# MLP products of a two-layer encoder as pairs of 64-row products in the two row halves of TensorE's array

## The chip, the core and the metric

The kernel runs on one core of a Trainium2 chip. The metric is the device time of the whole program in microseconds (us). The core's engines are TensorE (PE in the profile, its weight loads PEld), VectorE (DVE), ScalarE (ACT), GpSimd (POOL) and SyncE (SP, which here only issues transfers); each works through its own list of instructions and waits on semaphores for the others.

## What is computed

A two-layer encoder trunk on one sequence of 512 tokens, model width 1024, MLP width 4096, all in float32. Each layer is a mixer (layer 0: sparse attention beside gated linear attention; layer 1: stick-breaking attention) and then an MLP. The change touches the MLP alone:

```python
def squared_relu_mlp(n, w_up, w_down):
    return jnp.square(jax.nn.relu(n @ w_up)) @ w_down

# in each of the two layers
h = h + mixer(rmsnorm(h, g_mix[layer]), ...)
h = h + squared_relu_mlp(rmsnorm(h, g_ffn[layer]), w_up[layer], w_down[layer])
```

## The kernel before

The activations lie feature-major: a tile is 128 features on the partitions by all 512 tokens, so `h` is eight tiles and the MLP's hidden layer 32. One product on TensorE takes 128 x 128 weights as the operand that stays and a 128 x 512 tile as the operand that streams, and adds into one PSUM bank of 128 x 512 float32. For accuracy every float32 operand x is split into two tiles of the type float32r, hi and lo with hi + lo = x, and a product is made in three passes, hi·hi, hi·lo and lo·hi (`mm3`). ScalarE makes hi by a copy, VectorE makes lo by a subtraction (`split`).

Weights come in blocks of 128 x 1024 (half a megabyte): `plan` lists them in the order in which they are used, SP loads `raw`, ScalarE makes `whi` and VectorE `wlo`, with three buffers of each. `proj_fm` takes one block and makes eight `mm3`, 24 products, into one bank.

`mlp` runs in two halves of the hidden layer. For each of 16 hidden tiles f it calls `proj_fm` on the eight normed tiles of `h`, and the bank goes through ReLU (ScalarE), a square (VectorE) and a split. Then for each of the eight output tiles d it calls `proj_fm` twice on the 16 hidden tiles (48 products in one bank), VectorE multiplies the bank by the norm's factor `r2` and adds it to `h[d]`. In the second half `nxt(d)` follows: the norm's split for layer 1, or the store of the output. That is 2 x (16 x 24 + 8 x 48) = 1536 products in one MLP and 3072 in the two, all of one shape. The factor `r2` comes from `mean_fm`: a sum of squares is gathered tile by tile on POOL (`sum_squares`) and summed over the partitions by two products with a tile of ones, `ones_r`, which stand among the first products of the MLP.

The order of the instructions on each engine isn't that of the code. Each call is recorded by `Program.add`, and `Program.issue` makes a list schedule from the costs in `Program.cost`: of the instructions whose inputs are there, an engine takes the one of the highest priority. All instructions are issued from one recording line, so every row of the profile names line 307. Names in the rows: `bank` is a PSUM bank, `sl` one of 67 general tiles of 128 x 512, `h` the residual stream, and `sl,whi` a product that streams an `sl` tile against hi weights.

Of the kernel before, what the change touches and what calls it, by code (L numbers as in the profile page):

```python
# [14 lines left out]
AF = mybir.ActivationFunctionType  # L15
# [3 lines left out]
P = 128  # L19
# [30 lines left out]


def plan():
    """The weight blocks in the order in which the tensor engine takes them."""
    out = []

    def tm(w, c0):
        for k in range(0, KT, 2):
            out.append(("tm", w, k, c0))

    def fm(w, c0, k0=0, nk=KT):  # L60
        out.append(("fm", w, k0, c0, nk))

    def mlp(layer):
        for half in range(2):
            for f in range(16):
                fm(("w_up", layer), (half * 16 + f) * P)
            for d in range(KT):
                for q in range(2):
                    fm(("w_down", layer), d * P, half * 16 + q * 8)

    ab = ("w_in_ab", 0)
    out.append(("misc",))
    fm(ab, O_QB)
    fm(ab, O_QB + P)
    fm(ab, O_KB)
    fm(ab, O_KB + P)
    tm(ab, O_IQ)
    tm(ab, O_VB)
    tm(ab, O_KA)
    for i in range(4):  # L80
        fm(ab, O_OG + i * P)
    tm(ab, O_QA)
    tm(ab, O_VA)
    for half in (4, 0):
        for d in range(0, KT, 2):
            out.append(("fm2", ("w_out_ab", 0), half, d * P))
    mlp(0)
    c = ("w_in_c", 0)
    fm(c, 0)
    fm(c, D)  # L90
    tm(c, 2 * D)
    for h in range(1, HC):
        if h == 4:
            tm(c, 2 * D + 512)
        fm(c, h * P)
        fm(c, D + h * P)
    for half in (0, 4):
        for d in range(0, KT, 2):
            out.append(("fm2", ("w_out_c", 0), half, d * P))
    mlp(1)  # L100
    return out
# [25 lines left out]
    return np.ascontiguousarray(table), np.ascontiguousarray(np.concatenate(masks, 1).astype(np.float32))  # L127

class Program:
    """Collects the instructions of the kernel and issues them in the order of a list schedule.  # L130

    Each engine takes, of the instructions whose inputs are there by the time it is free, the one of the
    highest priority (program order, moved by `ahead`). An order is kept between two instructions that touch
    the same tile unless both only read it, and a tile takes a place of its tag when its first instruction
    is issued and leaves it after its last.
    """

    LATENCY = 0.14
    TO_TENSOR = 0.27
# [40 lines left out]

    @staticmethod
    def box(a):
        """The partitions and the columns that an access touches; of a PSUM bank, all columns."""
        pitch, parts = a.ap[0]
        first, column = divmod(a.offset, pitch) if pitch else (0, 0)
        if a.space == bass.MemoryType.PSUM or not pitch:
            return (0, 128), (0, 1 << 30)
        low = column + sum(min(0, st * (n - 1)) for st, n in a.ap[1:])
        high = column + sum(max(0, st * (n - 1)) for st, n in a.ap[1:])
        return (first, first + parts), (low, high + 1)  # L190

    def cost(self, engine, name, outs, ins):
        """Engine time in us."""
        out = outs[0]
        n = max(math.prod(a.shape[1:]) for a in outs + ins)
        if name == "dma_start":
            return 0.45 if engine == "sync" else 1.04
        if engine == "tensor":
            n = math.prod(out.shape[1:])
            if ins[0].dtype == R:  # L200
                return max(n / 2400 + 0.0025, 0.107)
            return max(n / 1200, 0.107) if name == "transpose" else max(n / 600, 0.16)
        psum = any(a.space == bass.MemoryType.PSUM for a in ins)
        if engine == "scalar":
            small = sum(1 for a in ins[1:] + outs[1:])
            return 0.00084 * n + (0.05 if psum else 0.09) + 0.093 * small + (4.2 if name == "silu" else 0)
        if engine == "vector":
            fast = not psum and (name in ("memset", "tensor_copy", "tensor_scalar"))
            return 0.065 + n * (0.00052 if fast else 0.00104)
        return 0.1 + n * (0.0009 if name == "memset" else 0.0023)  # L210

    def issue(self):
# [18 lines left out]
        order = []  # L231

        def need(i):
            """When there is room for the tiles that instruction i is the first to touch; None: not yet known."""
            when = est[i]
            want = {}
            for t, tag in ops[i]["tiles"].items():
                if t not in placed:
                    want[tag] = want.get(tag, 0) + 1
            for tag, n in want.items():  # L240
                kind = tag.split("_")[0]
                spare = self.reserve.get(kind, 0) if i - first >= self.window.get(kind, 0) else 0
                if len(places[tag]) < n + spare:
                    return None
                when = max(when, places[tag][n - 1])
            return when
# [66 lines left out]
def body(ctx: ExitStack, tc, xT, wch, wgu, small, table, masks, out, tap=None):  # L313
# [52 lines left out]
    gq_a, gk_a = sm[:, 39:71], sm[:, 71:103]  # L366

    def split(src, hi, lo, scale=None):
        """hi + lo = src (times scale), both exact as float32r."""
        if scale is None:  # L370
            A.activation(hi, src, AF.Copy)
            V.tensor_tensor(lo, src, hi.bitcast(F), OP.subtract)
# [26 lines left out]
        return ready.pop(i)  # L399

    def mm3(dst, lh, rh, first, last):
        """One product in three float32r passes."""
        (lhi, llo), (rhi, rlo) = lh, rh
        T.matmul(dst, lhi, rhi, start=first, stop=False, skip_group_check=True)
        T.matmul(dst, lhi, rlo, start=False, stop=False, skip_group_check=True)
# [2 lines left out]
    def proj_fm(act, dst, first=True, last=True):  # L408
        hi, lo = weights()
        for k in range(8):  # L410
            c = slice(k * P, k * P + P)
            mm3(dst, (hi[:, c], lo[:, c]), (act[k][0], act[k][1]), first and k == 0, last and k == 7)

    def proj_fm2(act, dsts):
        hi, lo = weights()
# [39 lines left out]
        return y  # L455

    def column_sums(x):
        """The sum over the partitions, on every partition."""
        xh, xl = sl(R), sl(R)
        split(x, xh, xl)  # L460
        pb = ps_bank()
# [19 lines left out]
    def mlp(n, acc, nxt):  # L481
# [6 lines left out]
        for half in range(2):  # L488
            act = []
            for f in range(16):  # L490
                dst = acc_bank()
                proj_fm(n, dst)
                a = sl()
                ah, al = sl(R), sl(R)
                A.activation(a, dst, AF.Relu)
                V.tensor_tensor(a, a, a, OP.mult)
                split(a, ah, al)
                act.append((ah, al))
            for d in range(KT):
                dst = acc_bank()  # L500
                proj_fm(act[:8], dst, True, False)
                proj_fm(act[8:], dst, False, True)
                a = sl()
                V.tensor_tensor(a, dst, r2, OP.mult)
                V.tensor_tensor(h[d], h[d], a, OP.add)
                if half == 1:
                    nxt(d)
# [3 lines left out]
            T.transpose(dst[:, i * P:i * P + P], s, ident)  # L511

    def weighted(dst, v, pT):
        """dst[d, t] = sum over keys s <= t of v[s, d] p[t, s]; pT[i] holds key tile i, queries from tile i on."""
        for i in range(NT):
            mm3(dst[:, i * P:], v[i], pT[i], i == 0, i == NT - 1)

    def turn(p):
        """p[j][t, s] of query tile j -> pT[i][s, t] of key tile i, split."""
        res = []  # L520
        for i in range(NT):
            pt = ps_bank()
# [5 lines left out]
            res.append((ph[:, :w], pl[:, :w]))  # L528
        return res

    # the tensor engine's clock rises while it is busy
    V.memset(ones, 1.0)
    onesR = const.tile([P, P], R, name="ones_r")
    V.tensor_copy(onesR, ones)
# [1 line left out]
    for _ in range(WARM):  # L536
        T.matmul(bank[:, 0:P], onesR, onesR, start=True, stop=True, skip_group_check=True)

    # ------------------------------------------------------------------ layer 0
    n = {}  # L540
    acc = sl()
    parts = [load(0), load(1)]
# [16 lines left out]
    vf = mean_fm(acc)  # L559
    rF = rsqrt(vf, S, sl)  # L560

    # index keys (64 rows), gate input (16), index weights (8)
    bank = acc_bank()
    proj_fm(n, bank)
    mf = sl()
# [4 lines left out]
    A.activation(mi, pt.rearrange("p (t c) -> p t c", t=NT), AF.Copy)  # L570

    def rope(x4, cos, sin, t1):
        """x4 [P, a, 2, half] rotated in place; cos, sin broadcastable to the same shape."""
        V.tensor_tensor(t1, x4[:, :, ::-1, :], sin, OP.mult)
        V.tensor_tensor(x4, x4, cos, OP.mult)
        V.tensor_tensor(x4, x4, t1, OP.add)
# [1 line left out]
    def tabI(tb, t):  # L578
        return tb[:, t].rearrange("p (two c) -> p two c", two=2)[:, None].to_broadcast([P, IH, 2, 8])

    # gated linear attention: projections, gates
    qb, kb = [], []
    for dst, sc_ in ((qb, DK ** -0.5), (kb, 1.0)):
        for p in range(2):
# [18 lines left out]
        G.memset(z, 0.0)  # L603
        lg.append(z)

    # index keys
    rt = tiny.tile([P, NT, 2, 8], F, name="rt_ik")
    ik4 = mi[:, :, 0:16].rearrange("p t (two c) -> p t two c", two=2)
    rope(ik4, cosI.rearrange("p t (two c) -> p t two c", two=2),
# [11 lines left out]
        iqs[t] = sl()  # L621
        A.activation(iqs[t], iq_ps[t], AF.Copy, scale=rT[:, t:t + 1])

    # index scores
    sc = {}
    for t in (1, 2, 3):
        nk = (t + 1) * P
# [33 lines left out]
        split(vb_ps[t], vh, vl, rT[:, t:t + 1])  # L661
        vb[t] = (vh, vl)

    # scores of all pairs s <= t, by the level at which s and t part
    # att[pair][t // 2][s, (t, head, query)] for the query tiles' own keys
    att = []
    for p in range(2):
        a = [sl(), sl()]
# [9 lines left out]
                                pd[:, t * 256:t * 256 + 256].rearrange("p (t c) -> p t c", t=2),  # L678
                                ident[:, None, :].to_broadcast([P, 2, P]), OP.mult)
    kl = [[sl() for _ in range(2)] for p in range(2)]  # L680
    # queries of both heads of a pair side by side, zero outside the head's own rows
    qx = [[sl() for _ in range(2)] for p in range(2)]
    for p in range(2):
        for b in range(2):
# [57 lines left out]
                    split(pl, ah, al)  # L742
                    off256[p, hh] = (ah, al)

    # the selection: TOPK // 8 rounds of eight maxima
    sel = {0: chunkR}
    with prog.ahead(-LATER):
        for t in (1, 2, 3):
# [10 lines left out]
            V.tensor_scalar(sl_t[:, :nk], wk[:, :nk], 1.0, -NEG, OP.subtract, OP.mult)  # L759
            sel[t] = sl_t[:, :nk]  # L760

    # sparse attention: keys, queries with norm, gain and rotation
    def qk_heads(gain, gain_col):
        """The gain of the rotated dims goes into the rotation's tables, that of the others into the split."""
        ct, st = (sl()[:, 0:P].rearrange("p (t c) -> p t c", t=NT) for _ in range(2))
        V.tensor_tensor(ct, cosA, gain[:, None, :].to_broadcast([P, NT, 32]), OP.mult)
        V.tensor_tensor(st.rearrange("p t (two c) -> p t two c", two=2), sinA.rearrange("p t (two c) -> p t two c", two=2),
# [135 lines left out]

    mlp(n2, acc2, into_layer1)

    # ------------------------------------------------------------------ layer 1
    n = n1
    vt = mean_tm(acc1)
    rT = rsqrt(vt, NT, lambda: tn(NT, "rt", 4))
# [126 lines left out]
```

## Time and profile before

| what | value |
|---|---|
| time, median of 3 runs | 1230.16 us (1228.16 to 1230.54) |
| span of the profiled execution, first to last instruction | 1228.2 us |
| median of the runs less that span | 1.96 us |
| PE busy, share of the span | 99% |
| PEld, DVE, ACT, POOL busy | 82%, 60%, 45%, 4% |
| mean granted TensorE clock, share of 2.4 GHz | 0.996 |
| read from HBM | 106.07 MB, 88 GB/s over the span |

The profiled execution has no time of its own beside its span; the runs say what a whole execution takes. Matmul rows overlap, since their ends are modelled: the distance from start to start says what one costs, not its duration.

### The profile page before, as it was taken

What the parts mean: (1) busy time and instruction counts of PE and PEld (TensorE: products, weight loads), DVE (VectorE), ACT (ScalarE), POOL (GpSimd) and SP (SyncE); (2) the same over time, 40 slices, a digit from 0 to 9 for tenths busy, and PEclk for the clock granted to TensorE, in tenths of its full rate; (3) what the DMA queues carried; (4) which work ended last, traced back from release to release, by engine and by line L of the source; (5) the groups of instructions that cost most, each with busy time, mean ns of one, the idle gap of its engine ahead of it and who ended that gap; (6) DMA issues with size and microseconds to landing.
All of it is one profiled execution on the core that took longest, in us unless ns stands there. A gap on an engine that the chain in (4) does not pass through costs nothing.

```text
span 1228.2 us, 14610 instructions
## 1 busy us (share of the span) xinstructions
PE 1212.7 (99%) x5638; PEld 1007.6 (82%) x5638; DVE 733.8 (60%) x1203; ACT 554.0 (45%) x989; POOL 54.7 (4%) x54
## 2 busy tenths in 40 slices
PE   9999999999999999999999999999899999999998
PEld 7788788888888888888888888888688888888886
DVE  6899999856443334444446797898744433444332
ACT  6582575635442223442335796895543321343220
POOL 2102000003000000000110000000300000000000
PEclk9999999999999999999999999999899999999999
DMA  6311212123233233233232212211223232233330
GB/s 228 100 59 49 69 52 86 53 70 102 89 100 103 88 101 102 87 103 100 90 103 86 77 60 70 86 53 52 90 99 103 88 102 100 89 103 101 105 129 26
DMA packets 31350, 109.12 MB, mean 89 GB/s; under 512 B 3632, under 2 KB 3648, under 8 KB 31280
## 3 DMA queue, kind: packets, MB, share of 16 engines
q1 hardware_dynamic: 31104, 107.55, 26.7%
q8 instruction: 44, 0.72, 0.2%
q0 software_dynamic: 176, 0.64, 0.1%
q14 instruction: 26, 0.21, 0.1%
HBM read 106.07 MB, written 2.10 MB: 88 GB/s over the span
## 4 chain that ended last, share of the span: by engine, by line
PE 84%; DVE 11%; ACT 2%; issue 2%; DMA 0%; POOL 0%; POOLq 0%; DVEq 0%
PE bank L307 84%; DVE sl L307 8%; ACT sl L307 2%; DVE wlo L307 2%; DVE m L307 1%; DVE h L307 0%; ACT whi L307 0%; DMA tbl<-table 0%; DVE mx L307 0%; POOL sl L307 0%; POOLq L1031 0%; DVE rt_iq L307 0%; DVE og L307 0%; DVE den L307 0%; DVE rt_a L307 0%
## 5 line engine op out<-in xcount | busy, mean ns | idle before, releaser
L307 PE MATMUL bank<-sl,whi 128*128 128x512 f32 x2704 | 844.3, 392 | 3.1 <-DVE sl L307 2.8
L307 PEld LDWEIGHTS bank<-sl,whi 128*128 128x128 f32 x2704 | 509.6, 189 | 110.2 <-DVE sl L307 5.1
L307 PE MATMUL bank<-sl,wlo 128*128 128x512 f32 x1352 | 529.4, 392 | 0.0
L307 ACT ACTIVATE whi<-raw 128x1024 fp32r<-128x1024 f32 (+1 forms) x199 | 209.3, 1052 | 447.4 <-PE bank L307 404.1
L307 DVE TENSOR_TENSOR wlo<-raw,whi 128x1024 fp32r<-128x1024 f32 (+1 forms) x199 | 241.1, 1212 | 265.4 <-ACT whi L307 265.0
L307 PEld LDWEIGHTS bank<-sl,wlo 128*128 128x128 f32 x1352 | 255.0, 189 | 52.6 <-DVE wlo L307 0.3
L307 ACT ACTIVATE sl<-sl 128x512 fp32r<-128x512 f32 (+5 forms) x315 | 163.1, 552 | 135.1 <-DVE sl L307 125.5
L307 DVE TENSOR_TENSOR sl<-sl 128x512 fp32r<-128x512 f32 (+5 forms) x268 | 158.6, 608 | 53.2 <-ACT sl L307 53.0
L307 DVE TENSOR_TENSOR sl<-bank,sl 128x512 f32<-128x512 f32 (+5 forms) x134 | 70.5, 557 | 122.2 <-PE bank L307 112.6
L307 PE MATMUL bank<-whi,sl 128*128 128x512 f32 x432 | 138.9, 395 | 0.0
L307 ACT ACTIVATE sl<-bank 128x512 f32<-128x512 f32 (+7 forms) x268 | 122.2, 501 | 32.8 <-PE bank L307 30.2
L307 PE MATMUL bank<-sl 128*128 128x128 f32 (+5 forms) x608 | 100.2, 312 | 3.1 <-DVE sl L307 2.6
L307 PEld LDWEIGHTS bank<-sl 128*128 128x128 f32 (+1 forms) x608 | 85.9, 193 | 12.9 <-issue 3.3
L307 PEld LDWEIGHTS bank<-whi,sl 128*128 128x128 f32 x432 | 81.0, 189 | 16.0 <-issue 0.3
L307 PE MATMUL bank<-wlo,sl 128*128 128x512 f32 x216 | 85.1, 394 | 0.0
L307 POOL TENSOR_TENSOR sl<-sl 128x512 f32<-128x512 f32 (+1 forms) x35 | 46.3, 1325 | 820.4 <-ACT sl L307 607.4
L307 PEld LDWEIGHTS bank<-wlo,sl 128*128 128x128 f32 x216 | 40.6, 188 | 7.9
L307 DVE SCALAR_TENSOR_TENSOR sl<-sl 128x512 f32<-128x512 f32 (+2 forms) x61 | 39.7, 663 | 6.2 <-ACT sl L307 5.2
L307 DVE SCALAR_TENSOR_TENSOR sl<-bank,sl 128x512 f32<-128x512 f32 (+3 forms) x52 | 28.5, 563 | 9.4 <-PE bank L307 7.2
L307 PE MATMUL bank<-tbl,sl 128*128 128x128 f32 x184 | 29.6, 276 | 2.8 <-DVE sl L307 2.5
L307 DVE SCALAR_TENSOR_TENSOR sl<-h,sm,sl 128x512 fp32r<-128x512 f32 x32 | 29.4, 928 | 3.2 <-ACT sl L307 3.2
L307 PEld LDWEIGHTS bank<-tbl,sl 128*128 128x128 f32 x184 | 22.2, 140 | 10.3 <-ACT sl L307 3.4
(79 smaller groups left out, 389.0 us busy)
## 6 DMA issues: line engine op xcount, KB each, us to landing
raw<-wch SPq DMA_DIRECT2D x195, 512.0 KB, 3.4
h<-xT SPq DMA_DIRECT2D x8, 256.0 KB, 6.1
out_dram<-h SPq DMA_DIRECT2D x8, 256.0 KB, 2.0
raw<-wch SPq DMA_DIRECT2D x4, 256.0 KB, 6.2
tbl<-table POOLq DMA_DIRECT2D x1, 384.0 KB, 5.0
sl<-masks POOLq DMA_DIRECT2D x1, 224.0 KB, 5.4
sm<-small SPq DMA_DIRECT2D x1, 51.5 KB, 1.9
wg<-wgu POOLq DMA_DIRECT2D x1, 16.0 KB, 5.5
```

Of the source, the lines that this page charges most:

```text
L307: self.program.add(self.name, what, lambda: fn(*args, **kw), outs, ins)
```

## The change

`mlp` calls a new function, `proj_rows`, in the place of `proj_fm`. It cuts the contraction of every product into rows 0 to 63 and rows 64 to 127: two products of 64 x 128 weights by 64 x 512 columns, one on each half of the array's rows, each with a bank of its own. So an MLP has two banks per output tile in the place of one, 3072 products of 128 rows become 6144 of 64 rows, and the two banks are added behind them: ScalarE copies the first to an `sl` tile, VectorE adds the second. ReLU, and the multiplication by `r2`, then read that tile and no longer a bank. The schedule's costs change too: a float32r product is costed at n/2400 + 0.0133 us (at least 0.109) where it was n/2400 + 0.0025 (at least 0.107), and half of that if it has 64 rows. Docstrings and comments were taken out as well, which changes no instruction; the diff leaves them out.

```diff
@@ Program.cost
             if ins[0].dtype == R:
-                return max(n / 2400 + 0.0025, 0.107)
+                return max(n / 2400 + 0.0133, 0.109) / (2 if ins[0].shape[0] == 64 else 1)
@@ beside proj_fm
+    def proj_rows(act, dsts, first=True, last=True):
+        hi, lo = weights()
+        halves = (slice(0, 64), slice(64, P))
+        for k in range(8):
+            c = slice(k * P, k * P + P)
+            for i, (w, x) in enumerate(((hi, 0), (hi, 1), (lo, 0))):
+                for r, dst in zip(halves, dsts):
+                    T.matmul(dst, w[r, c], act[k][x][r], start=first and k == 0 and i == 0,
+                             stop=last and k == 7 and i == 2, skip_group_check=True)
@@ mlp
             for f in range(16):
-                dst = acc_bank()
-                proj_fm(n, dst)
+                dsts = acc_bank(), acc_bank()
+                proj_rows(n, dsts)
                 a = sl()
                 ah, al = sl(R), sl(R)
-                A.activation(a, dst, AF.Relu)
+                A.activation(a, dsts[0], AF.Copy)
+                V.tensor_tensor(a, a, dsts[1], OP.add)
+                A.activation(a, a, AF.Relu)
                 V.tensor_tensor(a, a, a, OP.mult)
                 split(a, ah, al)
                 act.append((ah, al))
             for d in range(KT):
-                dst = acc_bank()
-                proj_fm(act[:8], dst, True, False)
-                proj_fm(act[8:], dst, False, True)
+                dsts = acc_bank(), acc_bank()
+                proj_rows(act[:8], dsts, True, False)
+                proj_rows(act[8:], dsts, False, True)
                 a = sl()
-                V.tensor_tensor(a, dst, r2, OP.mult)
+                A.activation(a, dsts[0], AF.Copy)
+                V.tensor_tensor(a, a, dsts[1], OP.add)
+                V.tensor_tensor(a, a, r2, OP.mult)
                 V.tensor_tensor(h[d], h[d], a, OP.add)
```

On PE, at the entry of layer 1's MLP, before: the last products of its first hidden tile (`sl_1713` and `sl_1714` are hi and lo of the seventh normed tile, `sl_1716` and `sl_1717` of the eighth), then the two products with `ones_r` among those of the second hidden tile.

```order
L307 MATMUL bank_1725<-sl_1714,whi_1700 128x512
L307 MATMUL bank_1725<-sl_1713,wlo_1701 128x512
L307 MATMUL bank_1725<-sl_1716,whi_1700 128x512
L307 MATMUL bank_1725<-sl_1717,whi_1700 128x512
L307 MATMUL bank_1725<-sl_1716,wlo_1701 128x512
L307 MATMUL bank_1732<-sl_1681,whi_1711 128x512
L307 MATMUL bank_1721<-sl_1719,ones_r_87 128x512
```

And on PE at the same place with the change (`sl_1761` and `sl_1762` are the seventh normed tile, `sl_1764` and `sl_1765` the eighth; the shape printed is the output's, so 64-row products read 128x512 too).

```order
L307 MATMUL bank_1773<-sl_1762,whi_1748 128x512
L307 MATMUL bank_1774<-sl_1762,whi_1748 128x512
L307 MATMUL bank_1769<-sl_1767,ones_r_87 128x512
L307 MATMUL bank_1773<-sl_1761,wlo_1749 128x512
L307 MATMUL bank_1774<-sl_1761,wlo_1749 128x512
L307 MATMUL bank_1773<-sl_1764,whi_1748 128x512
L307 MATMUL bank_1774<-sl_1764,whi_1748 128x512
L307 MATMUL bank_1769<-sl_1768,ones_r_87 128x512
L307 MATMUL bank_1773<-sl_1765,whi_1748 128x512
L307 MATMUL bank_1774<-sl_1765,whi_1748 128x512
L307 MATMUL bank_1773<-sl_1764,wlo_1749 128x512
L307 MATMUL bank_1774<-sl_1764,wlo_1749 128x512
```

What moved: the two halves of each product stand beside each other, with a bank each, and the first product with `ones_r` now stands ahead of five products (five pairs) that stood ahead of it before. Layer 0's MLP has the same pattern, and in both MLPs the two `ones_r` products are the only ones of 128 rows among the pairs.

On DVE, the last instructions of the program, before and then with the change (`sl_1723` and `sl_1771` are `r2`).

```order
L307 TENSOR_TENSOR wlo_2067<-raw_2065,whi_2066 128x1024
L307 TENSOR_TENSOR sl_2068<-bank_2061,sl_1723 128x512
L307 TENSOR_TENSOR h6_82<-h6_82,sl_2068 128x512
L307 TENSOR_TENSOR sl_2070<-bank_2069,sl_1723 128x512
L307 TENSOR_TENSOR h7_83<-h7_83,sl_2070 128x512
```

```order
L307 TENSOR_TENSOR sl_2163<-sl_2163,bank_2156 128x512
L307 TENSOR_TENSOR sl_2163<-sl_2163,sl_1771 128x512
L307 TENSOR_TENSOR h6_82<-h6_82,sl_2163 128x512
L307 TENSOR_TENSOR sl_2166<-sl_2166,bank_2165 128x512
L307 TENSOR_TENSOR sl_2166<-sl_2166,sl_1771 128x512
L307 TENSOR_TENSOR h7_83<-h7_83,sl_2166 128x512
```

Each output tile has an addition more on DVE, which waits for a copy on ACT that is new too.

## Rows read from the trace of the kernel before

**Rows 1.** The page: busy time of the engines, and the chain that ended last.

```profile
PE 1212.7 (99%) x5638; PEld 1007.6 (82%) x5638; DVE 733.8 (60%) x1203; ACT 554.0 (45%) x989; POOL 54.7 (4%) x54
...
PE 84%; DVE 11%; ACT 2%; issue 2%; DMA 0%; POOL 0%; POOLq 0%; DVEq 0%
```

**Rows 2.** The view of waits, PE alone: us in total, times, longest.

```profile
PE bank L307 <- DVE sl L307: 8.0, 8, 2.2
```

**Rows 3.** Busy time by stretch, most of layer 0's MLP: us, then PE, PEld, DVE, ACT, POOL, clock, DMA.

```profile
297.00:612.00 315.00, 315.00 (x1391) 260.98 (x1391) 133.41 (x155) 103.99 (x134) 5.92 (x4) 1.00 0.30 97
```

**Rows 4.** What touches PSUM banks, 300 to 600 us: duration ns min/median/max, first and last start.

```profile
L307 PE MATMUL bank<-sl,whi x884: 388/390/390, 299.8 to 599.9; 128*128 128x512 f32 x177
...
L307 PE MATMUL bank<-sl,wlo x441: 388/390/390, 300.2 to 599.4; 128*128 128x512 f32 x147
L307 ACT ACTIVATE sl<-bank x31: 576/582/582, 302.1 to 552.3; 128x512 f32<-128x512 f32 x31
L307 DVE TENSOR_TENSOR sl<-bank,sl x12: 691/692/692, 388.4 to 595.1; 128x512 f32<-128x512 f32 x12
```

**Rows 5.** Busy time from 878 to 883 us; the clock column is the eighth.

```profile
878.00:883.00 5.00, 5.00 (x12) 3.94 (x13) 3.66 (x5) 3.07 (x5) 0.00 (x0) 0.50 0.30 106
```

**Rows 6.** Timeline of PE in that stretch: start us, duration us, instruction.

```profile
878.96 0.63 PE L307 MATMUL bank<-sl,wlo 128*128 128x512 f32 x1
...
880.67 0.63 PE L307 MATMUL bank<-sl,wlo 128*128 128x512 f32 x1
```

**Rows 7.** Timeline of three products in layer 0's MLP and the last one's weight load.

```profile
599.64 0.62 PE L307 MATMUL bank<-sl,whi 128*128 128x512 f32 x2
599.87 0.19 PEld L307 LDWEIGHTS bank<-sl,wlo 128*128 128x128 f32 x1
600.09 0.39 PE L307 MATMUL bank<-sl,wlo 128*128 128x512 f32 x1
```

**Rows 8.** PE by form, 122.07 to 123.22 us.

```profile
L307 PE MATMUL bank<-sl 64*128 64x256 f32 x8 | 1.1, 389 | 0.0
```

**Rows 9.** PE by form, 39.7 to 41.6 us.

```profile
L307 PE MATMUL bank<-sl,wg 16*128 16x512 f32 x4 | 2.0, 613 | 0.0
```

**Rows 10.** Timeline of PE where products of 128 and of 64 rows meet.

```profile
92.54 0.39 PE L307 MATMUL bank<-whi,sl 128*128 128x512 f32 x1
92.86 0.49 PE L307 MATMUL bank<-sl 64*128 64x128 f32 x2
...
119.49 0.50 PE L307 MATMUL bank<-wlo,sl 128*128 128x512 f32 x1
119.83 0.40 PE L307 MATMUL bank<-whi,sl 128*128 128x512 f32 x1
```

**Rows 11.** Groups of DVE instructions by form, 300 to 600 us: busy us, mean ns.

```profile
L307 DVE TENSOR_TENSOR wlo<-raw,whi 128x1024 fp32r<-128x1024 f32 x55 | 67.3, 1224 | 110.3 <-ACT whi L307 110.3
L307 DVE TENSOR_TENSOR sl<-sl 128x512 fp32r<-128x512 f32 x32 | 22.2, 693 | 21.7 <-ACT sl L307 21.7
```

**Rows 12.** Timeline of the program's end, all engines.

```profile
1223.42 0.39 PE L307 MATMUL bank<-sl,wlo 128*128 128x512 f32 x1
1223.85 0.69 DVE L307 TENSOR_TENSOR sl<-bank,sl 128x512 f32<-128x512 f32 x1 [9.46 <-PE bank L307]
1224.58 0.69 DVE L307 TENSOR_TENSOR h<-h,sl 128x512 f32<-128x512 f32 x1
```

**Rows 13.** Timeline at the entry of layer 1's MLP, PE, ACT and POOL.

```profile
873.29 3.94 POOL L307 TENSOR_TENSOR sl<-sl 128x512 f32<-128x512 f32 x2 [1.81 <-ACT sl L307]
...
873.68 0.40 PE L307 MATMUL bank<-sl,wlo 128*128 128x512 f32 x1
...
876.14 0.50 PE L307 MATMUL bank<-sl,whi 128*128 128x512 f32 x1 [1.83 <-DVE sl L307]
...
877.26 0.63 ACT L307 ACTIVATE sl<-sl 128x512 fp32r<-128x512 f32 x1 [2.98 <-POOL sl L307]
...
877.95 0.80 PE L307 MATMUL bank<-sl,ones_r 128*128 128x512 f32 x1 [0.61 <-ACT sl L307]
```

## The prediction

> **What bounds the kernel now.** I read the page first: PE is busy 99% of the span, and the chain that ended last is PE for 84% [rows 1]. Busy says little of matmuls, whose ends are modelled, so I went to the waits: all that PE waits for others is some ten microseconds, 8.0 us of it for VectorE, in eight places [rows 2]. In the MLP it waits for nothing: in 315 us PE is busy 315, VectorE 133 and ScalarE 104 [rows 3]. So the MLP costs what its products cost from start to start. From 299.8 to 599.9 us there are 884 + 441 = 1325 products [rows 4], so the distance is 300.1 / 1324 = 0.2267 us. 3072 of them make 696 us of the 1228.2: the change works on 57% of the kernel, and everything hangs on what a pair of 64-row products costs against 0.2267 us.
>
> **What the 0.2267 is made of.** A product streams 512 columns. In a stretch with the granted clock at 0.50, which is 1.2 GHz [rows 5], four products take 880.67 - 878.96 = 1.71 us, 0.4275 each [rows 6]: 512 columns at 1.2 per ns are 0.4267, so at that clock the columns are all there is, weight loads included. At 2.4 GHz the columns would be 0.2133, and 0.2133 + 0.0133 = 0.2267 is measured. So at the full clock 13.3 ns per product aren't columns. Over 3072 products that is 40.9 us: the most that any regrouping can win here. The loads aren't late: one of 0.19 us starts at 599.87, as the second of two products from 599.64 on does, and is done at 600.06, 0.03 us before the product that it is for [rows 7].
>
> **The change, part by part.**
>
> *Two products of 64 rows in the place of one of 128.* Each half still streams 512 columns, so a pair can't be under 0.2133 us. Do the halves run at the same time? In plain float32 they do: eight products of 64 rows by 256 columns, four for each half, keep PE busy for 1.1 us with a mean of 0.389 [rows 8], so their starts are (1.1 - 0.389) / 7 = 0.10 us apart. One alone would take more: four products of 512 columns in that type are (2.0 - 0.613) / 3 = 0.46 us apart on average [rows 9], 0.23 for 256 columns. A pair takes 0.20 and a single one 0.23, so two cost as much as one, weight loads included. That type streams at most 512 columns in some 0.43 us, the rate at which no extra time shows with 128 rows either [rows 6], so these rows can't show what becomes of the 13.3 ns. Nothing in the trace has 64 rows at 2.4 columns per ns. Bounds for a pair: 0.2133 us from below (-40.9 us in all), twice 0.2267 from above, if float32r products of two halves don't overlap (+696 us). Which row is nearest? The one of the same type, rate and column count, with 128 rows. The 13.3 ns come with each product that streams and loads weights at the full rate, and vanish at half the rate with all 128 rows in use; so they follow the rate and not the rows. Each half streams at that rate and loads its own 128 columns of weights once per pair. I take 0.2267 us per pair: **0 us**.
>
> *Changes between 128 and 64 rows.* From a product of 128 rows and 512 columns to one of 64 rows the start comes after 92.86 - 92.54 = 0.32 us in the place of 0.227, and on the way back the first product of 128 rows takes 119.83 - 119.49 = 0.34 [rows 10]. So a change costs 0.09 us ahead of the first product of the new kind and 0.11 behind it, 0.2 in all. The order of the changed program has per MLP one change at the entry, four at the two `ones_r` products, and one at the exit, which the last MLP lacks: 11 x 0.2 = **+2.2 us** (0 if all fall into waits, 2.2 if none).
>
> *The second bank.* 64 hidden and 32 output tiles have 96 copies more on ScalarE and 96 additions more on VectorE. A read of a bank on ScalarE is 0.58 us, an addition on VectorE with a bank 0.69 [rows 4]. That is 56 us and 66 us in the two MLPs, 28 and 33 in each, on engines that are idle for 211 and 182 of 315 us [rows 3]: hidden. For one hidden tile, 24 x 0.2267 = 5.4 us on PE, VectorE then has one weight split of 1.22 us and three operations of 0.69 [rows 11, 4], 3.3 us: it keeps up. The cover would go if a pair cost under some 0.14 us, which is below the bound. With eight banks PE is three hidden tiles, 16 us, ahead of a pair of banks that waits for its readers. At the exit of layer 0's MLP the next stage streams seven finished tiles first, 21 x 0.227 = 4.8 us, over a chain that gets 1.3 us longer. **0 us.**
>
> *The program's end* has no cover. Before, the last product is followed by one multiplication and one addition of 0.69 us [rows 12]. Now a copy of 0.58 us and an addition of 0.69 come ahead, with one more handover, about 0.05 us by the step from the first to the second there (1224.58 - 1223.85 - 0.69 = 0.04): **+1.3 us**.
>
> *The entry of layer 1's MLP.* PE works in order. The first `ones_r` product starts at 877.95, behind POOL's sum of squares, which ends at 877.23, and ScalarE's split of it [rows 13]. Before, PE did five products in that wait: the one at 873.68, the next, the one at 876.14 and two behind it. In the changed order `ones_r` stands ahead of those five, so they come behind 877.95: 5 x 0.227 = 1.1 us, or 5 x 0.4275 = 2.1 at the clock of 0.50, which is granted from about there [rows 5]. I take **+1.5 us** (0 if the sum comes earlier in the new order, 2.1 at most). Layer 0's entry has the same order with hardly a wait: nothing.
>
> *The rest of the order* in the mixers is made anew, because the costs changed. All of PE's waits are some 10 us, and I see no reason for a sign: 0, within 4 either way.
>
> *Sum:* 2.2 + 1.3 + 1.5 = 5.0 us on the span of 1228.2 makes 1233.2. The median of the runs lies 1.96 above that span: **1235 us**, own range 1230 to 1241. A measurement here can tell about 0.2%, 2.5 us, from no change.
>
> **Rivals.**
>
> *A: the 13.3 ns go, wholly or in good part* (ends on the other side). If one half's columns run on while the other changes its weights, or the extra is a matter of rows, a pair nears 0.2133: 1235.2 - 40.9 = 1194; with half of it, 1215. It decides as soon as 1.6 ns per pair are gone (5.0 / 3072). For it: the float32 pairs show no extra that I can see [rows 8]. Against: they stream at half the rate, where 128 rows show none either [rows 6]. The Trainium skill speaks for it: "TensorE: Matmul & The Clock Gate", section "Part 3: Packing small matmuls — row/col tiling", says that a weight load overlaps products in flight only where the row group differs. By that rule loads would be exposed now and hidden in pairs, which gives A; the trace bears it out poorly, since loads already run under the product before them [rows 7]. Chance 0.28.
>
> *B: the forecast.* Chance 0.48.
>
> *C: a pair costs somewhat more than a product*, because two loads and two starts are now to be fitted into the time of one. If the second load costs both halves 13.3 ns too: +40.9, 1276 us; if half of that, +20.4, 1256. For it: the extra comes at the full rate, with one load per product. Against: the float32 pairs, with their two loads [rows 8]. Chance 0.16. That section of the Trainium skill has a rule for this as well: a group of tiles takes one product's time plus about 4 ns for each tile more, which by the page would be an estimated 12 us here; the row of float32 pairs is too coarse to show 4 ns.
>
> *D: the change doesn't do what it says*: halves in float32r follow each other, 1235 + 696 = 1931 us, or the pairs are granted the clock of 0.50, 3072 x 0.20 = 615 us more. For it: no pair in that type is in the trace. Against: the float32 pairs [rows 8]. Chance 0.08.
>
> **How the numbers follow.** The likeliest is B, 1235 us. Faster by over 0.2% are A and the best of B: 0.30. B's own range goes from no change to +11 us, its middle at twice the limit: 0.15 within 0.2%. The rest, 0.55, is slower: most of B, C, D. The range goes down to 1196, nearly all of A, and up to 1256, half of C; C's upper half and D, 0.16, and a little of A stay out.
>
> **What would show it.** In the MLP, the distance from one product to the next of the same half: 0.2267 us by B, under 0.225 by A, over 0.23 by C, 0.45 by D. VectorE near 52% and ScalarE near 41% busy there (rows of before plus the second bank's work), without PE waiting for them. Steps of 0.3 us at the `ones_r` products, five pairs behind 877.95 us, and 2.7 us from the last product to the last addition where it was 1.2. The prediction is wrong if the 13.3 ns per product belong to the number of rows, or if two loads at once cost time that one doesn't.

## The result, and the profile after

The changed kernel takes 1235.55 us (median of 4 runs, 1234.80 to 1236.67), the kernel before 1229.74 (4 runs, 1228.16 to 1230.54). The ratio of after to before is 1.0052, with an interval of 1.0038 to 1.0066: slower by half a per cent, 0.55 us from the forecast of 1235. The profiled execution has a span of 1234.9 us and took 1236.67, the longest of the four.

First the page of the kernel after, busy time of the engines:

```profile
PE 1214.9 (98%) x8710; PEld 1001.2 (81%) x8710; DVE 803.8 (65%) x1299; ACT 609.4 (49%) x1085; POOL 50.2 (4%) x54
```

There are 3072 products more than in [rows 1], and PE's busy time has moved by 2 us. VectorE has 70.0 us more and ScalarE 55.4, where 66 and 56 were forecast. Next what touches PSUM banks from 300 to 600 us in the kernel after, the stretch of [rows 4], and then busy time in the stretch of [rows 3] (us, then PE, PEld, DVE, ACT, POOL, clock, DMA):

```profile
L307 PE MATMUL bank<-sl,whi x1766: 386/386/497, 299.7 to 599.7; 64*128 64x512 f32 x197
...
L307 PE MATMUL bank<-sl,wlo x884: 386/386/394, 300.0 to 599.9; 64*128 64x512 f32 x177
...
L307 ACT ACTIVATE sl<-bank x43: 578/580/582, 301.8 to 589.6; 128x512 f32<-128x512 f32 x43
L307 DVE TENSOR_TENSOR sl<-sl,bank x43: 679/681/683, 302.5 to 590.8; 128x512 f32<-128x512 f32 x43
```

```profile
297.00:612.00 315.00, 315.00 (x2774) 259.49 (x2772) 164.51 (x198) 129.94 (x178) 4.37 (x4) 1.00 0.30 98
```

1766 + 884 = 2650 products of 64 rows are 1325 pairs, in the time in which 1325 products of 128 rows stood before: 300.2 / 1324 = 0.2267 us per pair. PE is busy for the whole stretch, VectorE for 52% of it (164.51 / 315) and ScalarE for 41%. Both readers of the banks are far from full, as forecast.

The timeline of PE after, where `ones_r` products of 128 rows stand between the pairs of layer 0's MLP, and its entry:

```profile
293.06 0.39 PE L307 MATMUL bank<-sl,wlo 128*128 128x512 f32 x1
293.37 0.73 PE L307 MATMUL bank<-sl,whi 64*128 64x512 f32 x4
...
297.61 0.61 PE L307 MATMUL bank<-sl,whi 64*128 64x512 f32 x4
298.15 0.50 PE L307 MATMUL bank<-sl,ones_r 128*128 128x512 f32 x1
298.59 0.50 PE L307 MATMUL bank<-sl,wlo 64*128 64x512 f32 x2
298.92 0.40 PE L307 MATMUL bank<-sl,whi 64*128 64x512 f32 x2
```

At the entry the step is 293.37 - 293.06 = 0.31 us. At `ones_r`, the steps are 0.32 (from the second pair of the row at 297.61, which starts at 297.84), 0.43 and 0.33, against 0.227 without a change: 0.40 us for the two changes. The forecast had 0.2 for each.

The timeline of the program's end after, all engines, as [rows 12]:

```profile
1228.75 0.39 PE L307 MATMUL bank<-sl,wlo 64*128 64x512 f32 x2
1229.17 0.60 ACT L307 ACTIVATE sl<-bank 128x512 f32<-128x512 f32 x1 [10.28 <-PE bank L307]
1229.80 0.69 DVE L307 TENSOR_TENSOR sl<-sl,bank 128x512 f32<-128x512 f32 x1 [8.74 <-ACT sl L307]
1230.52 0.69 DVE L307 TENSOR_TENSOR sl<-sl 128x512 f32<-128x512 f32 x1
1231.25 0.69 DVE L307 TENSOR_TENSOR h<-h,sl 128x512 f32<-128x512 f32 x1
```

From the last product to the start of the last addition it is 2.50 us, where it was 1.16: +1.34.

To see where the rest went I cut both traces at the same instructions: the first product of each MLP, the first product behind layer 0's MLP, and the last product of all. This table is worked out from the start times, not printed by a view; all in us, with the kernels of the experiments that it is needed for:

| stage | before | after | costs alone | pairs, old costs | two banks, 128 rows |
|---|---|---|---|---|---|
| layer 0's mixer | 289.27 | 293.37 | 291.94 | 289.64 | 289.68 |
| layer 0's MLP | 349.13 | 349.70 | 349.13 | 349.97 | 349.14 |
| layer 1's mixer | 229.17 | 235.29 | 235.20 | 229.45 | 229.19 |
| layer 1's MLP | 355.85 | 350.39 | 349.83 | 357.05 | 356.00 |
| from the last product | 4.79 | 6.13 | 4.79 | 6.13 | 5.59 |
| span | 1228.22 | 1234.88 | 1230.88 | 1232.24 | 1229.60 |

The MLP of layer 0, the changed work itself, has grown by 0.57 us. The mixers, whose products were not changed, have grown by 4.10 and 6.12, and layer 1's MLP has given 5.46 back. Small as the total is, its largest parts lie outside the changed products: in the mixers, where the prediction had put "0, within 4 either way", and in layer 1's MLP, where it had put +1.5.

### The profile page after: what moved, and what is told of

Its sections match the earlier page's. It is cut to its first block, busy times and chain, and to the rows that moved or that the text cites. A ratio compares the mean times of both kernels' runs of the same rounds, so it can differ in the third digit from the quotient of the medians.

```text
span 1234.9 us, 20945 instructions
## 1 busy us (share of the span) xinstructions
PE 1214.9 (98%) x8710; PEld 1001.2 (81%) x8710; DVE 803.8 (65%) x1299; ACT 609.4 (49%) x1085; POOL 50.2 (4%) x54
## 4 chain that ended last, share of the span: by engine, by line
PE 75%; DVE 17%; ACT 4%; issue 3%; DMA 0%; POOLq 0%; DVEq 0%; ACTq 0%
PE bank L307 75%; DVE sl L307 13%; ACT sl L307 3%; DVE wlo L307 2%; DVE m L307 1%; ACT whi L307 1%; DMA tbl<-table 0%; DVE mx L307 0%; DVE h L307 0%; DVE og L307 0%; POOLq L1046 0%; DVE rt_a L307 0%; DVE den L307 0%; DVE rt_iq L307 0%; DVE rho L307 0%
## 5 line engine op out<-in xcount | busy, mean ns | idle before, releaser
L307 PE MATMUL bank<-sl,whi 64*128 64x512 f32 (+1 forms) x4752 | 842.8, 388 | 0.5 <-DVE sl L307 0.3
L307 PEld LDWEIGHTS bank<-sl,whi 64*128 64x128 f32 (+1 forms) x4752 | 506.5, 185 | 108.0 <-DVE sl L307 1.6
L307 PE MATMUL bank<-sl,wlo 64*128 64x512 f32 (+1 forms) x2376 | 528.9, 388 | 0.0
L307 ACT ACTIVATE sl<-sl 128x512 fp32r<-128x512 f32 (+5 forms) x379 | 204.6, 568 | 190.3 <-DVE sl L307 183.2
L307 PEld LDWEIGHTS bank<-sl,wlo 64*128 64x128 f32 (+1 forms) x2376 | 254.2, 185 | 53.4 <-issue 0.5
L307 DVE TENSOR_TENSOR sl<-sl 128x512 f32<-128x512 f32 (+5 forms) x300 | 180.9, 617 | 93.6 <-ACT sl L307 91.9
L307 ACT ACTIVATE sl<-bank 128x512 f32<-128x512 f32 (+7 forms) x300 | 139.7, 516 | 42.6 <-PE bank L307 42.3
L307 DVE TENSOR_TENSOR sl<-sl,bank 128x512 f32<-128x512 f32 x96 | 65.4, 681 | 12.7 <-ACT sl L307 12.7
L307 DVE TENSOR_TENSOR sl<-bank,sl 128x512 fp32r<-128x512 f32 (+7 forms) x102 | 48.3, 513 | 7.4 <-ACT sl L307 7.1
L307 ACT ACTIVATE sl<-h,sm 128x512 fp32r<-128x512 f32 x32 | 22.8, 720 | 37.0 <-DVE h L307 35.4
```

Source lines behind the costliest of these rows:

```text
L307: self.program.add(self.name, what, lambda: fn(*args, **kw), outs, ins)
```

## Experiments

Two questions were open: whether the time comes from the pairs or from the new order that the changed costs make, and what the 13.3 ns per product belong to. Times stand beside those of the kernel before on the same chip.

**The schedule's costs alone.** Products and banks as before, only the line that tells the list schedule what a float32r product costs is the changed one:

```diff
-                return max(n / 2400 + 0.0025, 0.107)
+                return max(n / 2400 + 0.0133, 0.109) / (2 if ins[0].shape[0] == 64 else 1)
```

> The kernel before with the changed costs of the schedule alone: products of 128 rows, one bank. Its order up to the entry of layer 0's MLP is that of the changed kernel. Theory 1 (the slowdown is the new order of the mixers, a pair costs just what a product did): layer 0's MLP starts at 293.4 us as in the changed kernel, where before it was 289.3, and the time is 4 us or more above before, about 1234. Theory 2 (the slowdown is the pairs and the second bank; orders are worth nothing): 1230.

It took 1232.61 us (5 runs, 1232.37 to 1232.77) against 1228.41 (15 runs); ratio 1.0033, interval 1.0021 to 1.0046. So a cost in a planner, with nothing changed but the order of the instructions, makes the kernel slower by 4.2 us. In the trace the whole difference is in layer 0's mixer (+2.67); layer 1's mixer is 6.03 longer and its MLP 6.02 shorter. First PE's waits up to 289 us in the kernel before and with the costs alone (us, times, longest):

```profile
PE bank L307 <- DVE sl L307: 5.1, 5, 2.2
```

```profile
PE bank L307 <- DVE sl L307: 7.7, 6, 2.9
```

In layer 0's mixer PE waits 2.6 us longer for VectorE. Then busy time by stretch in layer 1, before (first fence) and with the costs alone:

```profile
800.00:840.00 40.00, 39.82 (x202) 32.46 (x201) 39.02 (x67) 31.66 (x70) 0.00 (x0) 1.00 0.20 65
...
875.00:885.00 10.00, 8.25 (x22) 6.08 (x23) 6.28 (x8) 3.81 (x6) 2.15 (x2) 0.66 0.31 107
```

```profile
800.00:840.00 40.00, 37.66 (x186) 29.91 (x185) 39.44 (x67) 34.20 (x73) 0.00 (x0) 1.00 0.20 61
875.00:885.00 10.00, 8.88 (x40) 6.93 (x39) 7.67 (x9) 5.40 (x8) 2.96 (x3) 1.00 0.34 105
```

From 800 to 840 us the new order loses 2.2 us of PE in the mixer, and at the entry of the MLP it does 40 products in ten microseconds instead of 22: the granted clock is 1.00 there instead of 0.66. PE's waits say where the time went. First the kernel before at the entry of its MLP (867.6 to 890 us) and the clock that follows there, then the mixer with the costs alone (641.1 to 876.2 us):

```profile
PE bank L307 <- DVE sl L307: 2.8, 3, 1.8
PE bank L307 <- ACT sl L307: 0.6, 1, 0.6
...
876.80:883.50 6.70, 6.09 (x15) 4.40 (x14) 4.24 (x6) 3.81 (x6) 0.43 (x1) 0.50 0.30 108
```

```profile
PE bank L307 <- ACT sl L307: 2.4, 5, 0.8
PE bank L307 <- DVE sl L307: 1.2, 3, 0.5
```

Before, PE waits 0.2 us in this mixer and 3.4 in the MLP; with the costs alone it is 3.6 and 1.1. The idle time has moved to an earlier place, and behind it the clock does not fall. In the MLP that gives back 2.3 us of waiting and up to 3.4 us of half clock (6.7 us at 0.50), which is most of the 6 us. Of the 6.03 us in the mixer, 3.4 are waits; the rest lies in the distances between its products and was not taken apart.

**Pairs with the old costs.** The changed kernel with the old constants in that line, so that the order of the mixers stays that of before:

```diff
-                return max(n / 2400 + 0.0133, 0.109) / (2 if ins[0].shape[0] == 64 else 1)
+                return max(n / 2400 + 0.0025, 0.107) / (2 if ins[0].shape[0] == 64 else 1)
```

> Pairs of 64 rows and two banks, with the costs of before (a pair costed as one product of before). Its order up to the entry of layer 0's MLP is that of before. Theory 1: layer 0's MLP starts at 289.3 us; what is left is the changes between 64 and 128 rows and the longer end, 2.2 + 1.3 us: about 1233, give or take 3 for the order of layer 1's mixer. Theory 2: 1235.5, as the changed kernel.

1233.11 us (5 runs, 1232.62 to 1234.21) against 1228.41; ratio 1.0040, interval 1.0027 to 1.0052. In the table the pairs alone cost 4.02 us of span: 1.34 at the end, 0.84 in layer 0's MLP, 1.19 in layer 1's, and 0.65 in the mixers. The clock falls at the entry of layer 1's MLP as before. The two parts add up in the spans, 2.66 + 4.02 = 6.68 against 6.66 measured, though not stage by stage, and in the medians they do worse: 4.2 + 4.7 against 5.8. The spans are of one execution each, and the one of the kernel before is among its longer ones: 1228.2 us, where the fifteen beside these two runs go from 1224.5 to 1228.6 with a median of 1226.6. So that the spans add up so closely is partly chance. Neither part alone is the result; both belong to it.

**The second bank alone.** 128 rows, old costs; even and odd blocks of the contraction go to two banks, with the copy and the addition of the changed kernel:

```diff
...
-                for r, dst in zip(halves, dsts):
-                    T.matmul(dst, w[r, c], act[k][x][r], start=first and k == 0 and i == 0,
-                             stop=last and k == 7 and i == 2, skip_group_check=True)
+                T.matmul(dsts[k % 2], w[:, c], act[k][x], start=first and k < 2 and i == 0,
+                         stop=last and k >= 6 and i == 2, skip_group_check=True)
```

> Products of 128 rows, even k into one bank and odd k into another, with the copy and the addition behind them and the costs of before: the second bank without the row halves. Theory 1: only the longer end shows, +1.3 us, about 1231, give or take 3 for the order of layer 1's mixer; no wait of PE in the MLPs. Theory 2, in the form that the second bank is what costs: 1234 to 1236.

1229.75 us (11 runs) against 1228.41; ratio 1.0008, interval 0.9999 to 1.0017. Layer 0's MLP is 0.01 us longer; only the end shows the second bank, with 0.80. It is hidden.

**One half alone.** Only rows 0 to 63 are multiplied in the MLP; the other half of its contraction, with its bank, copy and addition, is left out, so the output is another one; the costs are the old ones. A product then streams as many columns as one of a pair, with nothing beside it:

```diff
...
-                for r, dst in zip(halves, dsts):
-                    T.matmul(dst, w[r, c], act[k][x][r], start=first and k == 0 and i == 0,
-                             stop=last and k == 7 and i == 2, skip_group_check=True)
+                T.matmul(dsts[0], w[halves[0], c], act[k][x][halves[0]], start=first and k == 0 and i == 0,
+                         stop=last and k == 7 and i == 2, skip_group_check=True)
...
```

> Only the upper half of each pair, rows 0 to 63; the lower half of the MLP's contraction is left out, with its bank, copy and addition. If the 13.3 ns per product come with the rate and the type, as forecast: 0.2267 us from start to start, no change in the MLPs. If they belong to 128 rows in use, or if a second load in the pair has eaten a gain: 0.2133 to 0.22 us, and each MLP 10 to 20 us shorter.

One execution took 1531.5 us, which no theory had. Busy time by stretch, in layer 0's MLP and in layer 1's, the last row from the last wait of PE to the end of its work:

```profile
400.00:500.00 100.00, 100.00 (x443) 81.28 (x442) 38.75 (x44) 25.50 (x30) 0.00 (x0) 1.00 0.29 95
880.00:980.00 100.00, 100.00 (x235) 76.20 (x234) 26.58 (x33) 21.29 (x30) 0.00 (x0) 0.50 0.16 53
...
878.50:1525.00 646.50, 646.50 (x1513) 495.73 (x1513) 138.27 (x159) 101.06 (x127) 0.00 (x0) 0.50 0.15 50
```

In layer 0's MLP the question is answered: 443 products in 100 us, the same 0.2267 from start to start. The 13.3 ns come with half the rows and with no second product beside. In layer 1's MLP the granted clock is 0.50 to the end, and the products are some 0.427 us apart (646.5 / 1513), 512 columns at 1.2 GHz. Its entry is a wait in which the clock falls, as before; but with 128 rows, and with pairs, it rises again within some seven microseconds.

**The other half alone**, rows 64 to 127, to see whether that belongs to one half or to the one execution (the lines that differ from the run with the first half):

```diff
-                T.matmul(dsts[0], w[halves[0], c], act[k][x][halves[0]], start=first and k == 0 and i == 0,
+                T.matmul(dsts[0], w[halves[1], c], act[k][x][halves[1]], start=first and k == 0 and i == 0,
```

> Rows 64 to 127 alone; the upper half of the MLP's contraction is left out. If the fall of the granted clock at the entry of layer 1's MLP, from which the run with rows 0 to 63 alone never came back, belongs to one half in use: again 0.50 from about 876 us to the end, near 1530 us. If it was that execution's: full clock after some 7 us, near 1231. The distance at the full clock is 0.2267 us in both cases.

1531.47 us, and the same clock. Busy time by stretch of this kernel, and of the kernel of pairs with the old costs during its fall and behind it:

```profile
400.00:500.00 100.00, 100.00 (x443) 81.18 (x442) 38.74 (x44) 25.47 (x30) 0.00 (x0) 1.00 0.29 95
880.00:980.00 100.00, 100.00 (x234) 75.99 (x234) 26.59 (x33) 21.29 (x30) 0.00 (x0) 0.50 0.17 53
```

```profile
879.60:886.40 6.80, 6.80 (x27) 4.50 (x28) 5.05 (x8) 3.48 (x6) 0.00 (x0) 0.50 0.25 78
887.00:900.00 13.00, 13.00 (x118) 12.16 (x116) 6.26 (x8) 5.72 (x9) 0.00 (x0) 1.00 0.26 83
```

It does not matter which half: the stream of products in one half kept the full clock that it started with, and did not get it back once it had fallen, while the stream in both halves did.

**The halves one after the other.** Of each weight block first 24 products in the upper half, then 24 in the lower, all work done, with the old costs:

```diff
...
-        for k in range(8):
-            c = slice(k * P, k * P + P)
-            for i, (w, x) in enumerate(((hi, 0), (hi, 1), (lo, 0))):
-                for r, dst in zip(halves, dsts):
+        for r, dst in zip(halves, dsts):
+            for k in range(8):
+                c = slice(k * P, k * P + P)
+                for i, (w, x) in enumerate(((hi, 0), (hi, 1), (lo, 0))):
```

> The changed products, but all 24 of the upper half first and then all 24 of the lower one, with the costs of before. If halves overlap only where they stand beside each other in PE's order: 0.2267 us for each product of 64 rows, the MLPs twice as long, about 1930 us. If PE finds the work for the other half further on: 1235.

1732.13 us in one execution: by the start times the MLPs take 602 and 604 us, some 1.7 times those before and not twice, so neither theory had it. The clock has no part in it, at 0.999 on average. A timeline of PE at a change of half:

```profile
420.79 0.61 PE L307 MATMUL bank<-sl,whi 64*128 64x512 f32 x2
421.24 0.39 PE L307 MATMUL bank<-sl,wlo 64*128 64x512 f32 x1
421.25 0.83 PE L307 MATMUL bank<-sl,whi 64*128 64x512 f32 x4
421.81 0.49 PE L307 MATMUL bank<-sl,wlo 64*128 64x512 f32 x2
422.05 0.62 PE L307 MATMUL bank<-sl,whi 64*128 64x512 f32 x2
```

Within a half the products start 0.2267 apart; from 421.24 to 422.05 seven start in 0.81 us, 0.116 each. The pattern of whi, whi, wlo in each half tells them apart: where the half changes, the first products of the new half run beside the last three of the old one. It is not the list schedule that mixes them: but for the first blocks beside `ones_r`, PE's list holds 24 and 24 in turn in layer 0's MLP. The mean agrees: (24 x 0.2267 - 24 x 0.1961) / 0.2267 = 3.2, with 0.1961 the mean distance in that MLP (602.43 / 3072).

**The MLP in bfloat16, 128 rows.** High and low parts of the MLP's weights and inputs are bfloat16 in the place of float32r, so the products carry fewer bits of each operand; the rest is the kernel before. It asks whether the 13.3 ns belong to the type:

```diff
...
-        hi = wpool.tile([P, 1024], R, name="whi", tag="whi", bufs=ROOM["whi"])
...
+        dt = H if order[i][0] == "fm" and order[i][1][0] in ("w_up", "w_down") else R
+        hi = wpool.tile([P, 1024], dt, name="whi", tag="whi", bufs=ROOM["whi"])
...
-                ah, al = sl(R), sl(R)
+                ah, al = sl(H), sl(H)
...
```

> The kernel before with the MLP's hi and lo tiles, weights and activations, in bfloat16 in the place of float32r: 2 bytes per number where it was 4, less exact, the same columns and products of 128 rows. If the 13.3 ns come with float32r's wide operands: about 0.216 us or less from start to start, each MLP some 16 us shorter. If they come with any product that loads its weights at the full clock: 0.2267.

1196.6 us against 1226.24 in one execution each. What touches PSUM banks from 300 to 600 us, and busy time by stretch:

```profile
L308 PE MATMUL bank<-sl,whi x928: 379/379/379, 299.9 to 599.9; 128*128 128x512 bf16 x186
L308 PE MATMUL bank<-sl,wlo x464: 379/379/379, 299.7 to 599.5; 128*128 128x512 bf16 x155
```

```profile
297.00:597.00 300.00, 300.00 (x1392) 136.02 (x1390) 133.15 (x156) 103.59 (x133) 5.83 (x4) 1.00 0.32 102
```

1392 products make 300.2 / 1391 = 0.2158 us: 2.5 ns over the columns' 0.2133, where float32r has 13.3. A weight load takes 136.02 / 1390 = 0.098 us, where it was 0.188 [rows 3]. By the Trainium skill ("TensorE: Matmul & The Clock Gate", section "Back-to-back issue gap") the isolated gap from one warm product of N columns to the next is about N / 2.4 + 2.5 ns. The bfloat16 row, though a stream, agrees to 0.1 ns, and the float32r rows are 10.8 ns above it. The 131 ns that the same section gives for a sustained stream at N = 512 is in no run here: these products of 128 rows are 215.8 ns apart.

**Pairs in bfloat16**, the same edits on the changed kernel with the old costs:

```diff
...
-                return max(n / 2400 + 0.0133, 0.109) / (2 if ins[0].shape[0] == 64 else 1)
...
+                return max(n / 2400 + 0.0025, 0.107) / (2 if ins[0].shape[0] == 64 else 1)
...
-                ah, al = sl(R), sl(R)
+                ah, al = sl(H), sl(H)
...
```

> Pairs of 64 rows and two banks with the MLP's tiles in bfloat16 as in the run with products of 128 rows, costs of before. If a pair costs what a product of 128 rows does in any type: the same distance as there, within 1 ns. If the halves hide an extra only where there is one, or two loads cost more where products are shorter: a difference of more than 2 ns per pair.

1198.74 us in one execution. What touches PSUM banks from 300 to 600 us:

```profile
L308 PE MATMUL bank<-sl,whi x1855: 376/376/376, 299.8 to 599.8; 64*128 64x512 bf16 x186
L308 PE MATMUL bank<-sl,wlo x927: 376/376/376, 299.8 to 599.6; 64*128 64x512 bf16 x186
```

2782 products are 1391 pairs, and 300.0 / 1390 = 0.2158 us for each: a pair costs what one product costs in this type too.

**The bfloat16 kernel of 128 rows, timed**: the edit shown above.

> The same kernel as the run with the MLP's tiles in bfloat16 and 128 rows, timed. 3072 x 10.8 ns = 33 us less by the distance seen there (0.2158 against 0.2267): a ratio of 0.973 to 0.975 to before.

1195.39 us (4 runs, 1194.06 to 1196.54) against 1228.72 (7 runs); ratio 0.9730, interval 0.9712 to 0.9748. It beats both kernels, for the price of fewer bits in the MLP's operands.

## Why the prediction was right, point by point

**The pair, 0 us: right, and for the reason given.** It measured 0.2267 us in the kernel after and with the old costs. The argument was that the 13.3 ns follow the rate and not the rows. One half alone shows the second part of it directly: 0.2267 with 64 rows and no neighbour. The bfloat16 runs sharpen it: 10.8 of the 13.3 ns go with the type, at full rate, with 128 rows or pairs. What in float32r takes them stays open; the weight load is shorter in bfloat16 by 0.09 us as well, but it lies under the product before it in both types, so the runs don't tell load from stream.

**The rivals.** A needed a pair under 0.225, C one over 0.23, D 0.45 or a clock of 0.50: none is in the rows. Changing the row group (here, the half of the rows) at each product took no time away: 0.2267 us with it and without. The Trainium skill ("TensorE: Matmul & The Clock Gate", section "Part 3: Packing small matmuls — row/col tiling") says that a weight load overlaps products in flight only where the row group differs. That rule, which spoke for A, has nothing to give here, where loads run under the product before them already [rows 7]. The section's 4 ns for each further tile, cited at C, are seen inside a pair, whose second product starts 3 to 4 ns behind the first by the start times. They add nothing from one pair to the next. D's half about the clock was nearer than it looked: one half's stream stayed at 0.50 after a fall, the pairs' stream did not.

**Changes between 128 and 64 rows: right for each change, too large in the sum.** It is 0.40 us for two, forecast 0.4. But the 2.2 us of the sum came to about half: layer 0's MLP is 0.57 us longer after, and layer 1's 0.56 longer than with the costs alone (350.39 - 349.83). The kernels without pairs lose some 0.5 us at their first `ones_r` product too. In the kernel before it starts 0.61 us behind the product at 293.80, where 0.227 is the rule:

```profile
293.80 0.39 PE L307 MATMUL bank<-sl,wlo 128*128 128x512 f32 x1
294.41 0.50 PE L307 MATMUL bank<-sl,ones_r 128*128 128x512 f32 x1 [0.23 <-ACT sl L307]
```

**The second bank and the program's end: right.** 0.01 us in the MLP and 1.34 at the end, forecast 0 and 1.3. The end is the only place where those readers have no products over them.

**The entry of layer 1's MLP, +1.5: mis-sized, and read against the wrong surroundings.** In the kernel after, `ones_r` does wait for ScalarE ahead of its five pairs, but for 0.91 us:

```profile
884.12 0.49 PE L307 MATMUL bank<-sl,ones_r 128*128 128x512 f32 x1 [0.91 <-ACT sl L307]
```

It is the only wait of PE in that MLP. The forecast had left the other waits and the clock there as they were before, 3.4 us of waiting and some 6.7 us at 0.50. With the new order both are gone, and the stage is 5.46 us shorter instead of 1.5 longer. The busy time of 875 to 885 us after, to be read against 22 products at 0.66 before (most of the 61 have 64 rows):

```profile
875.00:885.00 10.00, 9.09 (x61) 6.66 (x59) 8.72 (x8) 4.77 (x8) 4.15 (x4) 1.00 0.31 106
```

The pairs with the old costs say nothing of this term: there `ones_r` stands behind the same products as before, and the 1.19 us of that MLP are for the greater part the changes at its two `ones_r` products.

**The rest of the order, 0 within 4: the step that was thin.** It gave no sign because PE's waits were few. The costs alone showed +2.7 us of span and +4.2 of time; in the kernel after the parts are +4.10 and +6.12 in the mixers, and -5.46 in the MLP behind. So that the total came within 0.55 us of the forecast is partly luck: the pairs' own price (4.0 of span) came out under the 5.0 of the sum, and the order's was not 0.

Layer 0's mixer is 1.43 us longer after than with the costs alone, although PE's order up to there is the same. Two rows of the same products say where that arose, first with the costs alone, then after:

```profile
14.60 0.39 PE L307 MATMUL bank<-sl,wlo 128*128 128x512 f32 x1
...
102.89 0.80 PE L307 MATMUL bank<-sl 128*128 128x128 f32 x5 [2.85 <-DVE sl L307]
```

```profile
15.54 0.40 PE L307 MATMUL bank<-sl,wlo 128*128 128x512 f32 x1
...
103.87 0.98 PE L307 MATMUL bank<-sl 128*128 128x128 f32 x3 [2.89 <-DVE sl L307]
```

The kernel after is 0.94 us behind by 15 us and 0.98 by 103 us. So two thirds of it arose at the program's start, where its products stay 0.43 us apart, the distance of half the clock, until 14.2 us, and those of the costs alone until 12.6. It is one execution, the longest of its four, and no trace of the others was kept. The same product starts at 14.62 us in the kernel before, so some 0.9 of the +4.10 is of this kind and not the order's. Most of the rest comes behind 103 us, with the clock. Busy time from 103 to 109 us, in the kernel before, after, and with the costs alone:

```profile
103.00:109.00 6.00, 4.81 (x26) 4.79 (x27) 4.87 (x14) 0.00 (x0) 1.74 (x3) 0.72 0.01 3
```

```profile
103.00:109.00 6.00, 5.13 (x21) 4.54 (x22) 6.00 (x16) 0.00 (x0) 0.73 (x1) 0.72 0.00 0
```

```profile
103.00:109.00 6.00, 5.29 (x33) 4.46 (x34) 6.00 (x16) 0.00 (x0) 0.75 (x2) 1.00 0.01 3
```

A clock of 0.72 over six microseconds is some 3.4 at half speed. The fall is no accident of the change: the kernel before has it too, and it is the costs alone that escape it, with a mean clock of 1.000 in all five executions. By the start times the lag is 2.3 us after the fall, but the costs alone then wait 0.71 us for VectorE where the kernel after does not wait, and 1.4 us are left. This is read from one execution of each and was not tested further.

## What to carry to other kernels

Before regrouping matmuls, find out what the time above the columns follows (type, clock, rows), with one stretch at each clock and a run at half the rows: here the number of rows had no part in it, and splitting the array won nothing. A cost constant in a scheduler is an edit of its own; time it by itself, since here it alone made the kernel 0.3% slower. Count the work that a change adds at the one place without cover, the end of the program.

## What the runs showed of the hardware that was not expected

After a fall, products in one half of the rows stayed at a granted clock of 0.50 to the end of the program, through 646 us of unbroken work, in both halves tried; pairs were back at 1.00 after 6.8 us. Products of one half start beside about three earlier ones of the other half that are still to come in their own stream, which makes 24 and 24 in turn some 1.7 times as long and not twice. And float32r products of 512 columns are 0.2267 us apart where bfloat16 ones are 0.2158, although a float32r weight load of 0.19 us is done before the product that it is for starts [rows 7].
